# Row maxima and a low pass as pairs of 64-row products in a hybrid attention layer

## The chip, the cores and the metric

One core of one Trainium2 chip runs the whole layer in one launch. The metric is the device time of one execution in microseconds (us). Five engines work from queues of their own, each in order: PE (matmuls; its weight loads are shown as PEld), DVE (elementwise and reductions), ACT (activations, copies), POOL (elementwise on SBUF), SP (issues DMAs). Time before: median 723.49 us of three runs, from 721.98 to 726.29.

## What is computed

One layer of a diffusion backbone: an adaLN-modulated RMSNorm, one input projection, two attention mixers side by side, gates, one output projection. There are 1024 latent tokens, 128 prompt tokens and 128 cached context tokens. Each mixer has 8 query heads of width 64 and 2 key heads, so that four query heads share a key head.

```python
# mixer A: every latent query sees the context and all latents
s = einsum('bqkgd,bskd->bkgqs', qblk, k_all) * d ** -0.5
p = softmax(s);  o_a = einsum('bkgqs,bskd->bqkgd', p, v_all)
# mixer B: context and the neighbours |i-j| <= 128, with one sink logit per head
s = concatenate([sink, s_ctx, s_band]); p = softmax(s)[..., 1:]
o_b = p_ctx @ v_ctx + p_band @ v_band
y = x + gate * (concatenate([o_a * silu(g_a), o_b * silu(g_b)]) @ w_out)
```

The softmax subtracts any number near the row's largest score; the result doesn't depend on which, as long as nothing overflows.

## The kernel before, in words

**Precision.** A number is split into a high part, rounded to fp32r, and a low part, the remainder in fp32r. A product of two split numbers is high x high + high x low + low x high: three fp32r matmuls, or fewer where two share the 128 rows of the array.

**Stages.** First norm, modulation and the gate columns of mixer A; then the queries of both mixers (`query`), keys and values (`key`, `put_keys`), the gate columns of mixer B; then the attention sweep with the output projection strewn into it. In `query` the four pairs of heads of a 128-token tile are transposed, split into `qo[0]` (high) and `qo[1]` (low), and written to DRAM by `put` on ACT's queue: high parts in rows 0 to 63 of `q_dram`, low parts in rows 64 to 127, for each key group 512 columns (four heads x 128 queries).

**Units and slots.** The sweep goes over units `(t, m, g)`: token tile, mixer, key group, in the order A, B, A, B for each tile. A unit of mixer A has nine slots, one for each block of 128 keys; a unit of mixer B has three or four (its window). In a slot the loop at the end calls, in this order: `tick` (what earlier slots put off with `later`), `scores` of this slot (mixer A: two matmuls and an exponential; mixer B: four transposes of ready weights), the work that is due by table, some output products, and `values` of the slot three earlier.

**Work that is due by table.** `u_load` brings a unit's queries as one tile `qt`, 128 rows x 512, five slots ahead. `max_items` finds the row maxima of a mixer A unit: for each of four heads and three groups of three key blocks one product of 384 columns (`pmx`, L858; `kha` holds each key's high part twice, in rows 0 to 63 and 64 to 127, so that queries' high and low parts both meet it) and one reduce on DVE (L859). `finish` then loads the queries' high part again (`qb`), negates the maxima, and `transpose` puts them (`ptm`, L877) as extra rows of `qb`. `weight_items` makes mixer B's weights in natural layout: for each head two products (L915 with the keys' high part, L916 with their low part, `klb`, again stored twice), a masked maximum with the sink on DVE (L919), the exponential with its sum on ACT (L905). Then come the inverses of the sums: reciprocal on DVE, a transpose on PE (`pti`, L967), a copy on ACT (L971).

`MX_AT` and `NAT_AT` are slots counted from the start of another unit: a mixer A unit's maxima lie in the mixer B slots ahead of the previous mixer A unit (-4 to -1) and in that unit's own slots (4 to 8); a mixer B unit's weights in the slots 0 to 3 of the mixer A unit before it. Units 0 and 2 take their maxima earlier, beside mixer B's gate products.

**Accumulators.** PSUM has eight banks of 512 fp32 columns. Two of tag A rotate: each call of `bank("A", ...)` takes the other one, and waits for that one's last reader. All products above (`pmx`, `sn`, `ptm`, `pti`) use tag A; scores use B, value sums C, output products D and E.

Of the kernel before, what the change touches and what calls it, by code (L numbers as in the profile page):

```python
# [39 lines left out]
LOADED = 4  # L40


NAT_AT = (0, 1, 2, 3)
NAT_FIRST = (0, 1, 2, 3)
MX_AT = (-4, -3, -2, -2, -1, 4, 5, 5, 7, 7, 8, 8)
MX_FIRST = (0, 1, 2, 2, 3, 4, 4, 5, 6, 6, 7, 8)
PH_DVE = 0
MX_END = 10
SPLIT_LAG = 2
# [58 lines left out]
def hybrid_step(ctx, tc, x_prompt, x_sample, cache_k_a, cache_v_a, cache_k_b, cache_v_b,  # L108
# [26 lines left out]


    ps = ctx.enter_context(tc.tile_pool(name="ps", bufs=1, space=PSUM))
    BANKS = {"A": 2, "B": 2, "C": 2, "D": 1, "E": 1}
    turn = {"mm": 0, "tr": 0}
# [411 lines left out]
    with tc.tile_pool(name="qt", bufs=2, side="right") as qt:  # L551
# [34 lines left out]
        def query(pq, m, t, tabs, n=1):  # L586

            nm = f"q{m}_{t}"
            pqv = pq.rearrange("p (h d) -> p h d", d=HD)
            v = {}  # L590

            def squares():
                sq = qt.tile([P, 8, HD], F32, tag="sq", name=f"sq{nm}")
                nc.scalar.activation(sq, pqv, AF.Square)  # L594
                ss = qt.tile([P, 8], F32, tag="ss", name=f"ss{nm}")
                nc.vector.tensor_reduce(ss, sq, axis=AX.X, op=ALU.add)
                v["r"] = rsqrt_mean(qt, ss, HD, 8, nm)

            def scale():
                qn = qt.tile([P, 8, HD], F32, tag="qn", name=f"qn{nm}")  # L600
                nc.vector.tensor_tensor(qn, pqv, v["r"].unsqueeze(2).to_broadcast([P, 8, HD]), op=ALU.mult)
                v["qn"] = qn
                if t:
                    v["rot"] = rope_products(qt, qn, 8, *tabs[m], t, nm)

            def rotated():

                qf = qt.tile([P, 4, 2, HD], F32, tag="qf", name=f"qf{nm}", bufs=3)
                out = qf.rearrange("p h g d -> p g h d")
                pair = lambda a: a.rearrange("p (g h) d -> p g h d", g=2)  # L610
                if t:
                    nc.vector.tensor_tensor(out, *(pair(a) for a in v["rot"]), op=ALU.add)
                else:
                    nc.vector.tensor_tensor(
                        out, pair(v["qn"]), gain4[:, 2 * m, :].unsqueeze(1).unsqueeze(1).to_broadcast([P, 2, 4, HD]),
                        op=ALU.mult)
                v["qf"] = qf

            def turned():
                ptq = bank_tr(f"pt{nm}")  # L620
                for h in range(4):
                    nc.tensor.transpose(ptq[:, P * h : P * h + P], v["qf"][:, h].rearrange("p g d -> p (g d)"),
                                        ident_r.bitcast(F32))
                qo = [qt.tile([P, 512], F32R, tag=f"qo{i}", name=f"qo{i}{nm}") for i in range(2)]
                nc.scalar.copy(qo[0], ptq)
                put(qo[0], 0)
                later(1, lambda: low(ptq, qo))

            def low(ptq, qo):
                nc.vector.tensor_tensor(qo[1], ptq, qo[0], op=ALU.subtract)  # L630
                later(1, lambda: put(qo[1], 1))

            def put(part, i):
                for g in range(2):
                    nc.scalar.dma_start(q_dram[t][m][64 * i : 64 * i + 64, 512 * g : 512 * g + 512],
                                       part[64 * g : 64 * g + 64].bitcast(F32))
# [197 lines left out]
    def u_load(i):  # L834
        t, m, g = units[i]
        more = i % QTS > 3
        qt_ = (qp2[0] if more else qp).tile([P, 512], F32R, tag="qt", name=f"qt{i}", bufs=QTS - 4 if more else 4)
        nc.sync.dma_start(qt_.bitcast(F32), q_dram[t][m][:, 512 * g : 512 * g + 512])
        qtile[i] = qt_

    def max_items(i):

        t, m, g = units[i]
        out = []

        def item(h, b):
            if h == 0 and b == 0:
                mxtile[i] = qs.tile([P, 4, 3], F32, tag="mx", name=f"mx{i}", bufs=3)
            mx = mxtile[i]
            lhs = qtile[i][:, P * h : P * h + P]  # L850
            pm = bank("A", f"pmx{i}_{h}_{b}")
            if t == 0:
                for h in range(4):
# [3 lines left out]
            else:  # L857
                nc.tensor.matmul(pm[:, 0:384], lhs, kha[:, g, 3 * b : 3 * b + 3, :], start=True, stop=True)  # L858
                nc.vector.tensor_reduce(mx[:, h, b : b + 1], pm[:, 0:384], axis=AX.X, op=ALU.max)  # L859

        def finish():
            qb_ = qp.tile([68, 512], F32R, tag="qb", name=f"qb{i}", bufs=2)
            nc.sync.dma_start(qb_[0:64, :].bitcast(F32), q_dram[t][m][0:64, 512 * g : 512 * g + 512])
            qbtile[i] = qb_
            mx = mxtile.pop(i)
            mn = m_nat[i // 2 % 2]
# [15 lines left out]
        for h in range(4 if t else 1):  # L882
            for b in range(3 if t > 0 else 1):
                out.append(lambda h=h, b=b: item(h, b))
        return out, finish

    def weight_items(i):
# [20 lines left out]
        def item(h):  # L908
            p0, p1_ = window(t)
            n = P * (p1_ - p0)  # L910
            if h == 0:
                first(n)
            lhs = qtile[i][:, P * h : P * h + P]
            s = bank("A", f"sn{i}_{h}")[:, 0:n]
            nc.tensor.matmul(s, lhs, khb[:, g, p0:p1_, :], start=True, stop=False)  # L915
            nc.tensor.matmul(s, lhs, klb[:, g, p0:p1_, :], start=False, stop=True)  # L916
            m0 = P if t == 1 else 0

            nc.vector.tensor_tensor_reduce(s, s, mask[:, m0 : m0 + n], -1.0, nsink[:, 4 * g + h : 4 * g + h + 1],  # L919
                                           op0=ALU.add, op1=ALU.min, accum_out=v["nm"][:, h : h + 1])  # L920
            later(1, lambda: exp(h, s, -1.0))

        def prompt():
            first(P)
# [55 lines left out]
        return ([lambda h=h: item(h) for h in range(4)] if t else [prompt]), finish  # L980


    wo_raw, wo_parts, wo_big = {}, {}, {}
# [231 lines left out]
    for i, (t, m, g) in enumerate(units):  # L1215
# [8 lines left out]
        else:  # L1224
            items, done = weight_items(i)
            at = [start[i - 1] + j for j in (NAT_AT if i > 1 else NAT_FIRST)] if t else [start[i] - PROMPT_LEAD]
            end = at[-1] + 1
# [95 lines left out]
```

## Time and profile before

| | us |
|---|---|
| median of three runs | 723.49 |
| lowest and highest run | 721.98, 726.29 |
| the profiled execution, first to last instruction (span) | 721.3 |
| first and last `ptm` of the sweep over latent tiles, from the start of the span | 353.4, 662.2 |
| one unit of mixer A and one of mixer B in it | 23.84 to 23.87 |

The profile is of one execution, and its time is the span; the page gives no other time for it. In its lists an instruction is named by line, engine, operation, and `out<-in` with the program's tile names without buffer numbers; `128*64` means 128 rows by 64 columns of the array, `128x512` partitions by elements, `x4` four of them merged. In a timeline the two figures ahead are start and length in us. A matmul's length is its latency; the next one begins sooner, so the distance between two starts tells what one costs. In brackets stands how long the engine was idle before, and what released it.

### The profile page before, as it was taken

How to read it: one execution, taken by the hardware profiler on the slowest of the kernel's cores; microseconds unless marked ns; L12 is line 12 of the kernel's file. 1: busy time of each engine (PE TensorE's matmuls, PEld its weight loads, DVE VectorE, ACT ScalarE, POOL GpSimd, SP SyncE). 2: the span in 40 equal slices, each digit the busy share in tenths (PEclk: the TensorE clock that was granted, in tenths of full speed). 3: DMA queues.
4: the chain of work that ended last, by engine and by line, in shares of the span. 5: the costliest groups of instructions: out<-in, count | busy, mean ns of one | idle time of the engine just before them, and what ended most of it. 6: DMA issues, size and time to landing. Idle time of an engine off the chain costs nothing. (4 is left out here: it accounts for less than half of the span.)

```text
span 721.3 us, 10622 instructions
## 1 busy us (share of the span) xinstructions
PE 698.3 (97%) x3524; PEld 559.7 (78%) x3524; DVE 457.6 (63%) x1007; ACT 411.7 (57%) x829; POOL 335.3 (46%) x355
## 2 busy tenths in 40 slices
PE   5999999999999999999999999999999999999997
PEld 2678988877777788977788888888888888887865
DVE  3466147875675872745866677577666775775653
ACT  5355411411232451158778877877787778877770
POOL 3456013332322340236666555655575557555751
PEclk9999999999999999999999999999999999999999
DMA  8961373348435115440321222121212221212323
GB/s 344 346 219 59 121 278 86 79 94 276 121 85 142 45 60 171 139 143 23 103 67 45 73 67 88 44 81 52 87 54 59 66 87 45 81 53 87 103 65 119
DMA packets 53159, 78.56 MB, mean 109 GB/s; under 512 B 6569, under 2 KB 25449, under 8 KB 52081
## 3 DMA queue, kind: packets, MB, share of 16 engines
q1 hardware_dynamic: 44928, 65.96, 28.1%
q10 hardware_dynamic: 8176, 11.94, 6.3%
q8 instruction: 28, 0.46, 0.3%
q14 instruction: 27, 0.21, 0.1%
HBM read 58.69 MB, written 19.18 MB: 108 GB/s over the span
## 5 line engine op out<-in xcount | busy, mean ns | idle before, releaser
L1108 POOL TENSOR_TENSOR pl<-pe,ph 128x512 fp32r<-128x512 f32 x130 | 167.6, 1292 | 144.7 <-DVE nm L919 67.5
L859 DVE TENSOR_REDUCE mx<-pmx 128x1 f32<-128x384 f32 x192 | 101.4, 552 | 59.5 <-PE pmx L858 58.1
L1100 ACT ACTIVATE pe<-st 128x512 f32<-128x512 f32 x146 | 86.8, 594 | 28.0 <-PE st L1098 27.1
L1104 ACT CAST ph<-pe 128x512 fp32r<-128x512 f32 x146 | 90.6, 621 | 4.8
L1118 PE MATMUL pv<-ph,v_hi 128*128 128x512 f32 x208 | 83.2, 400 | 2.2 <-DVE spare L1142 2.2
L1121 PE MATMUL pv<-pl,v_hi 128*128 128x512 f32 x208 | 82.6, 397 | 0.0
L173 POOL TENSOR_TENSOR rs_q<-ms_q,mhalf 128x8 f32<-128x8 f32 x18 | 34.8, 1931 | 82.1 <-DVE ms_q L171 82.1
L1189 PE MATMUL po<-wo,ogh 128*128 128x512 f32 x216 | 72.5, 394 | 0.2 <-DVE yt L1196 0.2
L919 DVE CUSTOM_DVE_ANT_0 sn<-sn,mask,nsink 128x512 f32<-128x512 f32 (+1 forms) x64 | 46.3, 724 | 38.3 <-PE sn L916 36.5
L858 PE MATMUL pmx<-kha,qt 128*128 128x384 f32 x192 | 61.0, 363 | 0.4 <-ACT pen L905 0.2
L1097 PE MATMUL st<-qt,kha 128*128 128x512 f32 x144 | 58.3, 405 | 1.5 <-ACT pe L1100 0.8
L1098 PE MATMUL st<-qb,kla 68*128 68x512 f32 x144 | 57.6, 400 | 1.1 <-DVE qb L878 1.1
L1120 PE MATMUL pv<-ph,v_lo 128*64 128x512 f32 x146 | 57.9, 396 | 0.0
L1121 PEld LDWEIGHTS pv<-pl,v_hi 128*128 128x128 f32 x208 | 39.4, 189 | 16.7 <-issue 0.2
L905 ACT ACTIVATE pen<-sn,nm 128x512 f32<-128x512 f32 (+2 forms) x72 | 45.0, 626 | 6.5 <-DVE nm L919 3.1
L1093 ACT CAST ph<-st 128x512 fp32r<-128x512 f32 x62 | 36.4, 587 | 19.9 <-PE st L1092 18.7
L1118 PEld LDWEIGHTS pv<-ph,v_hi 128*128 128x128 f32 x208 | 39.4, 189 | 10.5 <-ACT ogh L1154 2.4
L1189 PEld LDWEIGHTS po<-wo,ogh 128*128 128x128 f32 x216 | 40.0, 188 | 6.8 <-DVE yt L1196 0.6
L1094 DVE TENSOR_TENSOR pl<-st,ph 128x512 fp32r<-128x512 f32 x62 | 42.5, 686 | 2.3 <-ACT ph L1093 1.5
L1189 PE MATMUL po<-wo,ogl 128*128 128x512 f32 x108 | 42.6, 394 | 0.0
L594 ACT ACTIVATE sqq<-pq 128x512 f32<-128x512 f32 x18 | 10.8, 599 | 53.3 <-DMA qd<-qo0q 14.4
L858 PEld LDWEIGHTS pmx<-kha,qt 128*128 128x128 f32 x192 | 35.5, 190 | 6.2 <-DVE mx L859 1.4
(216 smaller groups left out, 1700.2 us busy)
## 6 DMA issues: line engine op xcount, KB each, us to landing
qt<-qd SPq DMA_DIRECT2D x36, 256.0 KB, 3.1
wm<-in_w_mod_ss_dram SPq DMA_DIRECT2D x8, 1024.0 KB, 5.1
qd<-qo0q ACTq DMA_DIRECT2D x36, 128.0 KB, 2.4
qd<-qo1q ACTq DMA_DIRECT2D x36, 128.0 KB, 2.4
sgl<-gd SPq DMA_DIRECT2D x36, 128.0 KB, 2.1
out_dram<-yt SPq DMA_DIRECT2D x17, 256.0 KB, 2.1
xn<-in_x_sample_dram SPq DMA_DIRECT2D x8, 512.0 KB, 7.0
wg<-in_w_mod_g_dram SPq DMA_DIRECT2D x4, 1024.0 KB, 7.9
```

Source lines behind the costliest of these rows:

```text
L858: nc.tensor.matmul(pm[:, 0:384], lhs, kha[:, g, 3 * b : 3 * b + 3, :], start=True, stop=True)
L859: nc.vector.tensor_reduce(mx[:, h, b : b + 1], pm[:, 0:384], axis=AX.X, op=ALU.max)
L919: nc.vector.tensor_tensor_reduce(s, s, mask[:, m0 : m0 + n], -1.0, nsink[:, 4 * g + h : 4 * g + h + 1], op0=ALU.add, op1=ALU.min, accum_ou ...
L1097: nc.tensor.matmul(s, kh, qtile[i], start=True, stop=False)
L1098: nc.tensor.matmul(s, kl, qbtile[i], start=False, stop=True)
L1100: nc.scalar.activation(pe, s, AF.Exp)
L1104: nc.scalar.copy(ph, pe)
L1108: nc.gpsimd.tensor_tensor(pl, pe, ph, op=ALU.subtract)
L1118: nc.tensor.matmul(pv, two, ph, start=(b == 0), stop=False)
L1120: nc.tensor.matmul(pv[0:64, :], vl, ph, start=False, stop=False)
L1121: nc.tensor.matmul(pv, two, pl, start=False, stop=last)
L1189: nc.tensor.matmul(po[n], a, wo_parts[KT * n + k][lo], start=(k == KS[0] and p == 0), stop=(k == KS[-1] and p == 2))
```

## The change

- In DRAM a query tile is now `[4, 64, 2, 256]`: two heads' high part, the same heads' low part, the next two heads' high part, their low part, in pieces of 256 numbers. `u_load` issues two DMAs: rows 0 to 63 of `qt` get the low part of heads 0 and 1 and the high part of heads 2 and 3, rows 64 to 127 the high part of heads 0 and 1 and the low part of heads 2 and 3. All full 128-row products are sums over the same pairs of rows as before.
- `halves(q)` names two heads, q and q + 2, and the row at which each one's high part starts: 64 and 0.
- The maxima of mixer A now take the queries' high part alone: one product over 64 rows for each of the two heads, at row 64 and at row 0 of the array, into two banks, and one reduce over both.
- Mixer B's product with the keys' low part takes the queries' high part alone, in the same pairs. The product with the keys' high part stays whole.
- The two banks of tag A are one tile, `two`. A pair writes both; single users still take turns.
- The tables have half as many entries: maxima in slots -4, -3, -2, 4, 6, 8, mixer B's weights in slots 0 and 2.

```diff
-NAT_AT = (0, 1, 2, 3)
-MX_AT = (-4, -3, -2, -2, -1, 4, 5, 5, 7, 7, 8, 8)
+NAT_AT = (0, 2)
+MX_AT = (-4, -3, -2, 4, 6, 8)
...
-    q_dram = [[dram.tile([P, 1024], F32, name=f"qd{t}_{m}") for m in range(2)] for t in range(NT)]
+    q_dram = [[dram.tile([4, HD, 2, 256], F32, name=f"qd{t}_{m}") for m in range(2)] for t in range(NT)]
...
+    two = ps.tile([P, 2, 512], F32, name="two")
     def bank(tag, name):
+        if tag == "A":
+            turn["A"] += 1
+            return two[:, turn["A"] % 2]
...
-        nc.sync.dma_start(qt_.bitcast(F32), q_dram[t][m][:, 512 * g : 512 * g + 512])
+        for a, parts in ((0, slice(1, 3)), (HD, slice(0, 4, 3))):
+            nc.sync.dma_start(qt_[a : a + HD].bitcast(F32).rearrange("d (s n) -> d s n", s=2),
+                              q_dram[t][m][parts, :, g, :].rearrange("s d n -> d s n"))
+    def halves(q):
+        return (q, HD), (q + 2, 0)
...
-                nc.tensor.matmul(pm[:, 0:384], lhs, kha[:, g, 3 * b : 3 * b + 3, :], start=True, stop=True)
-                nc.vector.tensor_reduce(mx[:, h, b : b + 1], pm[:, 0:384], axis=AX.X, op=ALU.max)
+            for n, (h, a) in enumerate(halves(q)):
+                nc.tensor.matmul(two[:, n, 0:384], qtile[i][a : a + HD, P * h : P * h + P],
+                                 kha[a : a + HD, g, 3 * b : 3 * b + 3, :], start=True, stop=True, tile_position=(a, 0))
+            nc.vector.tensor_reduce(mx.rearrange("p (n q) b -> p q b n", n=2)[:, q, b], two[:, :, 0:384], axis=AX.X,
+                                    op=ALU.max)
...
-            nc.tensor.matmul(s, lhs, khb[:, g, p0:p1_, :], start=True, stop=False)
-            nc.tensor.matmul(s, lhs, klb[:, g, p0:p1_, :], start=False, stop=True)
+            for j, (h, a) in enumerate(halves(q)):
+                nc.tensor.matmul(two[:, j, 0:n], qtile[i][:, P * h : P * h + P], khb[:, g, p0:p1_, :], start=True,
+                                 stop=False)
+            for j, (h, a) in enumerate(halves(q)):
+                nc.tensor.matmul(two[:, j, 0:n], qtile[i][a : a + HD, P * h : P * h + P], klb[a : a + HD, g, p0:p1_, :],
+                                 start=False, stop=True, tile_position=(a, 0))
```

The order of instructions at three places follows; line numbers of the changed kernel are larger by some 12 to 19. First PE, where mixer B's slots begin (first slot, up to the second one's maxima), before:

```order
L1092 MATMUL st_0_5536<-ident_r,pen_5339 128x128 x4
L858 MATMUL pmx_0_0_5545<-kha,qt_5437 128x384
L1118 MATMUL pv_5415<-ph_6_5473,v_hi 128x512
L1120 MATMUL pv_5415<-ph_6_5473,v_lo 64x512
L1121 MATMUL pv_5415<-pl_6_5474,v_hi 128x512
L967 MATMUL pti_5551<-ident_r,inv_5343 4x128
L1092 MATMUL st_1_5556<-ident_r,pen_5339 128x128 x4
L858 MATMUL pmx_0_1_5569<-kha,qt_5437 128x384
```

and PE in the same unit with the change:

```order
L1111 MATMUL st_0_5333<-ident_r,pen_5150 128x128 x4
L870 MATMUL two<-kha,qt_5244 128x384 x2
L1137 MATMUL pv_5223<-ph_6_5275,v_hi 128x512
L1139 MATMUL pv_5223<-ph_6_5275,v_lo 64x512
L1140 MATMUL pv_5223<-pl_6_5276,v_hi 128x512
L986 MATMUL two<-ident_r,inv_5154 4x128
L1111 MATMUL st_1_5352<-ident_r,pen_5150 128x128 x4
L870 MATMUL two<-kha,qt_5244 128x384 x2
```

The single products became pairs in the same places; the transpose of the inverses stays between two of them, all on the tile `two`. On DVE, from the last mixer A slot into the same mixer B slots, before:

```order
L859 TENSOR_REDUCE mx_5248<-pmx_3_1_5523 128x1
L859 TENSOR_REDUCE mx_5248<-pmx_3_2_5526 128x1
L954 RECIPROCAL inv_5343<-sum_5341 128x4
L859 TENSOR_REDUCE mx_5544<-pmx_0_0_5545 128x1
L1094 TENSOR_TENSOR pl_0_5538<-st_0_5536,ph_0_5537 128x512
L869 TENSOR_REDUCE m_5566<-mx_5248 128x4
L872 TENSOR_SCALAR m_nat_108<-m_5566 128x4
L859 TENSOR_REDUCE mx_5544<-pmx_0_1_5569 128x1
```

and DVE with the change:

```order
L872 TENSOR_REDUCE mx_5067<-two 128x2
L973 RECIPROCAL inv_5154<-sum_5152 128x4
L872 TENSOR_REDUCE mx_5341<-two 128x2
L1113 TENSOR_TENSOR pl_0_5335<-st_0_5333,ph_0_5334 128x512
L884 TENSOR_REDUCE m_5362<-mx_5067 128x4
L887 TENSOR_SCALAR m_nat_109<-m_5362 128x4
L872 TENSOR_REDUCE mx_5341<-two 128x2
```

Each reduce now reads two banks and gives two maxima. Last, PE in the second and third slot of a mixer A unit, with mixer B's scores, before:

```order
L1097 MATMUL st_1_5353<-qt_4853,kha 128x512
L1098 MATMUL st_1_5353<-qb_5268,kla 128x512
L915 MATMUL sn_1_5362<-khb,qt_5233 128x512
L916 MATMUL sn_1_5362<-klb,qt_5233 128x512
L1189 MATMUL po_0_5006<-wo_6_3231,ogh_5213 128x512
L1189 MATMUL po_0_5006<-wo_6_3230,ogl_5214 128x512
L1189 MATMUL po_0_5006<-wo_7_3255,ogh_5213 128x512
L1118 MATMUL pv_5324<-ph_2_5281,v_hi 128x512
L1121 MATMUL pv_5324<-pl_2_5282,v_hi 128x512
L1097 MATMUL st_2_5376<-qt_4853,kha 128x512
L1098 MATMUL st_2_5376<-qb_5268,kla 128x512
L915 MATMUL sn_2_5385<-khb,qt_5233 128x512
```

and PE there with the change:

```order
L1116 MATMUL st_1_5167<-qt_4704,kha 128x512
L1117 MATMUL st_1_5167<-qb_5086,kla 128x512
L1208 MATMUL po_0_4843<-wo_6_3200,ogh_5034 128x512
L1208 MATMUL po_0_4843<-wo_6_3199,ogl_5035 128x512
L1208 MATMUL po_0_4843<-wo_7_3218,ogh_5034 128x512
L1137 MATMUL pv_5135<-ph_2_5099,v_hi 128x512
L1140 MATMUL pv_5135<-pl_2_5100,v_hi 128x512
L1116 MATMUL st_2_5185<-qt_4704,kha 128x512
L1117 MATMUL st_2_5185<-qb_5086,kla 128x512
L929 MATMUL two<-khb,qt_5051 128x512 x2
L932 MATMUL two<-klb,qt_5051 128x512 x2
```

The second slot no longer has a head; the third has two, whose half products are the last pair of rows.

More of the change, by code (lines that the diff above doesn't have):

```diff
@@ L634, in put @@
                 for g in range(2):
[L635 to L636 removed]
+                    nc.scalar.dma_start(
+                        q_dram[t][m][i::2, :, g, :].rearrange("s d n -> d s n"),
+                        part[64 * g : 64 * g + 64].bitcast(F32).rearrange("d (s n) -> d s n", s=2))
             for d, f in zip(QUERY_LAST if (m, t) == (1, 0) else QUERY_AT, (squares, scale, rotated, turned)):
@@ L844, in max_items, with item @@
         out = []
-        def item(h, b):
-            if h == 0 and b == 0:
+        def item(q, b):
+            if q == 0 and b == 0:
                 mxtile[i] = qs.tile([P, 4, 3], F32, tag="mx", name=f"mx{i}", bufs=3)
             mx = mxtile[i]
-            lhs = qtile[i][:, P * h : P * h + P]
-            pm = bank("A", f"pmx{i}_{h}_{b}")
             if t == 0:
+                pm = bank("A", f"pmx{i}")
                 for h in range(4):
@@ L880, in transpose @@
                                     diag.unsqueeze(2).to_broadcast([4, 4, P]), op=ALU.mult)
-        for h in range(4 if t else 1):
-            for b in range(3 if t > 0 else 1):
-                out.append(lambda h=h, b=b: item(h, b))
+        for q in range(2 if t else 1):
+            for b in range(3 if t else 1):
+                out.append(lambda q=q, b=b: item(q, b))
         return out, finish
@@ L978, in rows @@
                                   r_dram[i // 2].rearrange("(c s) n -> s c n", s=2)[s : s + 1].to_broadcast([HD, 2, P]))
-        return ([lambda h=h: item(h) for h in range(4)] if t else [prompt]), finish
+        return ([lambda q=q: item(q) for q in range(2)] if t else [prompt]), finish
     wo_raw, wo_parts, wo_big = {}, {}, {}
@@ L1226, in hybrid_step @@
             at = [start[i - 1] + j for j in (NAT_AT if i > 1 else NAT_FIRST)] if t else [start[i] - PROMPT_LEAD]
-            end = at[-1] + 1
+            end = at[-1] + (2 if t else 1)
         if i >= LOADED:
```

27 lines of the change are left out of this document (14 added, 13 removed).

## The prediction

> **What bounds the kernel now.** I read the page's busy times first:
>
> ```profile
> PE 698.3 (97%) x3524; PEld 559.7 (78%) x3524; DVE 457.6 (63%) x1007; ACT 411.7 (57%) x829; POOL 335.3 (46%) x355
> ```
>
> Then the windows, over the query projections and over one whole period of the attention sweep (from one transpose of maxima, `ptm`, to the next):
>
> ```profile
> 105.00:205.00 100.00, 99.22 (x473) 77.02 (x472) 73.38 (x142) 26.93 (x48) 31.17 (x16) 1.00 0.49 137
> 520.22:544.09 23.87, 23.87 (x116) 19.18 (x115) 17.67 (x37) 18.74 (x37) 14.09 (x15) 1.00 0.27 85
> ```
>
> The columns are length, then busy time of PE, PEld, DVE, ACT and POOL, granted clock, DMA share, GB/s. PE is busy for the whole of a period and at full clock; ACT is next with 18.74 of 23.87 us. A period holds one unit of mixer A (nine slots) and one of mixer B (four). So PE's instructions set the time, and what is taken from them counts, as far as nothing else then makes PE wait. A busy PE is not yet proof of that, so I read the starts of neighbouring matmuls, which are the pace:
>
> ```profile
> 500.59 0.39 PE L915 MATMUL sn<-khb,qt 128*128 128x512 f32 x1
> 500.82 0.40 PE L916 MATMUL sn<-klb,qt 128*128 128x512 f32 x1
> ...
> 507.50 0.40 PE L1118 MATMUL pv<-ph,v_hi 128*128 128x512 f32 x1
> 507.73 0.40 PE L1120 MATMUL pv<-ph,v_lo 128*64 128x512 f32 x1
> 507.97 0.40 PE L1121 MATMUL pv<-pl,v_hi 128*128 128x512 f32 x1
> ...
> 508.68 0.51 PE L858 MATMUL pmx<-kha,qt 128*128 128x384 f32 x2
> 509.02 0.39 PE L1189 MATMUL po<-wo,ogl 128*128 128x512 f32 x1
> ```
>
> A matmul of 512 columns holds PE for 0.23 us (500.59 to 500.82), two of 384 columns for 0.34 (508.68 to 509.02), 0.17 each. The second figure of a row, 0.39, is latency and is not paid by the next one.
>
> **What the change takes from PE.** The twelve row-maximum products of a mixer A unit (L858, 384 columns) become six pairs, each half over 64 rows. If two halves run side by side, a pair costs 0.17 and a stagger, taken as 0.01: 0.18 in place of 0.34 to 0.35. Sixteen units with six pairs are 96 pairs, 96 x 0.16 = **15.4 us**. In mixer B two full low passes (L916) become one pair: 0.24 in place of 0.46 for 24 pairs of 512 columns, 0.16 less for the 8 pairs of 384 at the window's ends: 24 x 0.22 + 8 x 0.16 = **6.6 us**. Together 22.0 us.
>
> No row of this profile has a matmul at a row offset; the nearest are the column tiles of the gate rows, four at a time:
>
> ```profile
> 158.73 0.39 PE L250 MATMUL pq<-whiqb,h 128*128 128x512 f32 x1
> 159.05 1.92 PE L573 MATMUL pgate<-wg,sil32g 128*32 128x512 f32 x16
> 160.90 0.66 PE L622 MATMUL ptq<-ident_r,qfq 128*128 128x128 f32 x4
> 161.31 0.47 PE L248 MATMUL pq<-whiqb,h 128*128 128x512 f32 x1
> ```
>
> Sixteen products of 512 columns end within 1.92 us, though at 0.23 each they would hold PE for 3.7. So tiles at different positions do run together. The same rows show a price: the block begins 0.32 after the matmul ahead of it, 0.09 more than the usual pace, and a matmul whose weights were not loaded under the one ahead takes 0.47 (161.31) where its like takes 0.39 (158.73). Against this, the 128*64 product at 507.73 stands between 128*128 ones with 0.23 and 0.24 on either side: there a change of tile costs nothing. The block that pays has plain fp32 operands (`wg`, `sil32g`), the 128*64 product has fp32r ones (`ph`, `v_lo`), as the new pairs have. Bounds for a pair's extra cost are thus 0 (507.73) and, on both sides, 0.09 for the start and 0.08 for such a weight load in the open, 0.34 in all. I take 0, since the fp32r row is the nearer one.
>
> The Trainium skill ("TensorEngine Tiling (Array Packing)", Tiling Modes, Key Properties) says that changing the tiling mode drains the TensorE, which speaks against pairs strewn one by one among full products. By that rule the row at 507.73 should show a gap, and it does not; it is a column mode, though, and no row here shows a row mode. What a drain would do is the second rival.
>
> **What takes it back.** Both accumulators of tag A become one tile, `two`, and every pair fills both banks. Before, a product took the bank that its predecessor had not; now each use waits until the last reader of both is done. Where mixer B's slots begin, the orders printed above show what that does. The transpose of the inverses (`pti` before, `two<-inv` now) stands as close behind the maxima as it did, but now overwrites what their reduce still reads, and its copy must in turn end before the next pair. On DVE one reduce of 768 elements stands where one or two of 384 did, with the same subtraction (`pl`) and small steps between. The times of this place before the change (start, length), on PE:
>
> ```profile
> 514.50 0.51 PE L858 MATMUL pmx<-kha,qt 128*128 128x384 f32 x2
> ...
> 515.53 0.60 PE L1092 MATMUL st<-ident_r,pen 128*128 128x128 f32 x4
> 515.89 0.42 PE L858 MATMUL pmx<-kha,qt 128*128 128x384 f32 x1
> ...
> 516.86 0.27 PE L967 MATMUL pti<-ident_r,inv 128*4 128x128 f32 x1
> ...
> 517.32 0.42 PE L858 MATMUL pmx<-kha,qt 128*128 128x384 f32 x1
> ...
> 520.22 0.22 PE L877 MATMUL ptm<-ident_r,m_nat 128*4 128x128 f32 x1
> ```
>
> on DVE
>
> ```profile
> 514.87 1.02 DVE L859 TENSOR_REDUCE mx<-pmx 128x1 f32<-128x384 f32 x2 [0.97 <-PE pmx L858]
> 515.81 0.17 DVE L954 RECIPROCAL inv<-sum 128x4 f32<-128x4 f32 x1
> 516.35 0.56 DVE L859 TENSOR_REDUCE mx<-pmx 128x1 f32<-128x384 f32 x1 [0.37 <-PE pmx L858]
> 516.83 0.68 DVE L1094 TENSOR_TENSOR pl<-st,ph 128x512 fp32r<-128x512 f32 x1
> 517.42 0.16 DVE L869 TENSOR_REDUCE m<-mx 128x4 f32<-128x12 f32 x1
> 517.61 0.42 DVE L872 TENSOR_SCALAR m_nat<-m 128x4 fp32r<-128x4 f32 x1
> 517.95 0.55 DVE L859 TENSOR_REDUCE mx<-pmx 128x1 f32<-128x384 f32 x1
> ```
>
> and on ACT
>
> ```profile
> 517.17 0.25 ACT L971 COPY spare<-pti 4x128 f32<-4x128 f32 x1 [0.41 <-PE pti L967]
> ```
>
> What a longer reduce takes I read from the groups by form, of 384 and of 512 elements (mean ns behind the busy time):
>
> ```profile
> L859 DVE TENSOR_REDUCE mx<-pmx 128x1 f32<-128x384 f32 x192 | 101.4, 552 | 59.5 <-PE pmx L858 58.1
> ...
> L596 DVE TENSOR_REDUCE ssq<-sqq 128x8 f32<-128x512 f32 x18 | 12.3, 684 | 12.3 <-ACT sqq L594 12.1
> ```
>
> A reduce takes 0.55 us for 384 elements and 0.68 for 512, so about 0.95 for 768 (an estimate on that line). A reader starts 0.46 after a matmul whose weights load in the open (515.89 to 516.35), and a release reaches PE some 0.04 later. On the clock of these rows:
> 1. Pair at 514.50, reduce 514.89 to 515.84. The next pair gets there at 515.74 (one product fewer ahead) and goes at 515.88: waits 0.14.
> 2. Its reduce runs 516.34 to 517.30. `pti` gets there at 516.86 and goes at 517.34: waits **0.48**.
> 3. Its copy ended 0.56 after it began, now 517.90. The next pair, 0.46 behind `pti`, gets there at 517.80 and goes at 517.94: 0.14.
> 4. DVE does `pl`, the small maximum and `m_nat` until 518.41 (1.1 from one reduce to the next's start, as from 516.83 to 517.95), then the reduce until 519.36. From a pair to the next slot PE takes 0.97 (515.89 to 516.86), and 0.36 of transposes; it is there at 519.27 and goes at 519.40: 0.13.
> 5. Behind the next `pl` (0.57 until its follower starts) that reduce runs 519.93 to 520.88. PE takes 0.97 and two output products, gets to `ptm` at 520.83 and goes at 520.92: 0.09.
>
> That is 0.98 us a period (`ptm` 0.70 later than at 520.22, with two products fewer on the way). Behind the waiting products in PE's queue stand the value products, which nothing else delays, so the wait is paid in full. In every second period a tile's output is finished at this place:
>
> ```profile
> 538.42 0.69 DVE L1196 TENSOR_TENSOR yt<-po,yt 128x512 f32<-128x512 f32 x1
> 539.03 1.01 DVE L859 TENSOR_REDUCE mx<-pmx 128x1 f32<-128x384 f32 x2
> ```
>
> One period of 23.87 after 514.50 the pair stands at 538.37; its reduce starts at 539.03 and ends at 539.98, so step 1 costs 0.41 and all 1.25. Fourteen of the sixteen mixer A units have such pairs (the first two take their maxima beside the gate products, where nothing stands close): 14 x 1.12 = **15.7 us**.
>
> In mixer B's scores, two sink minima and two exponentials now follow one another on the same two banks, with two slots between. I count nothing there, since a whole slot without such a pair lies between; the upper bound is one more wait like step 2's, 0.48 x 16 = 8 us, the lower none. Shorter reduces in sum (six of 0.95 for twelve of 0.55) and the copies that DVE and ACT make are not on the path.
>
> The queries lie in memory in pieces of 256 numbers, where 512 stood together, and each tile is loaded by two DMAs in place of one. SP issues 36 more; the writes stand on ACT's queue as before. The cover is PE, busy for 99.22 of 100 us where they are written with DMA at 0.49, and a lead of five slots where they are read. Bounds are 0 and, should a landing be late once a unit, some 0.1 x 36 = 4 us; I take 0.
>
> **The sum.** 22.0 off, 15.7 back: 6.3 us less than the profiled 721.3, which is 715.0. The runs' median, 723.49, lies 2.2 above that span (the lowest of them, 721.98, 0.7), so on its scale 717.2.
>
> **Rivals.**
> *The waits are covered.* Should DVE's reduce cost hardly more than one of 384, or the waits overlap with ones that I count twice, only some 5 us come back: 706. Against it: step 2 needs only one row, 552 ns and its length. 0.08.
> *Each pair drains PE (slower).* At either end of a pair PE empties and loads weights in the open, as the fp32 blocks do: 0.18 + 0.34 = 0.52 in place of 0.35, and 0.57 in place of 0.46: 96 x 0.17 + 32 x 0.11 = 20 us more. Waits on the banks shrink to some 0.5 a period, 7 us. 723.5 + 27 = 750. It decides from 0.05 us a pair on, since 6.3 us over 128 pairs is no more than that. For it: 159.05; against it: 507.73. 0.20.
> *The change doesn't do what it says.* If the row halves run one behind the other, PE saves nothing, and the waits, a little smaller, remain: 0.9 x 14 = 13 us more, 736. If only the second half's weights are late (a load in the open is about 0.1, from four transposes in 0.36 at 515.53), a pair costs 0.28: some 9 us off, 15 back, 729. For both: no row pair is in this trace; against: sixteen column tiles in 1.92. Together 0.20.
>
> **How the numbers follow.** Forecast as summed, with 711 to 722 for its own range (waits of 0.8 to 1.4 a period), 0.52. With 0.08, 0.20 and 0.20 for the rivals: faster by over 0.5% means below 719.9, which is most of the forecast's case and the first rival, 0.47. Within 0.5%, about what a measurement of this kernel can tell from no change: the forecast's upper end and a part of the late weights, 0.18. Slower: 0.35. The range leaves out most of the draining case, and a little below: 707 to 744.
>
> **What would show it.** Right: two products of `two<-kha` starting within 0.02 us, and the next full one 0.18 later; PE idle about 0.5 us before `two<-inv`, released by DVE's reduce; a period of 23.2 to 23.7 us. Wrong: 0.3 us or more between the matmul ahead and a pair (drain); 0.1 or 0.17 between its halves; idle time before L929 released by ACT; reduces of 768 far from 0.95.

## The result, and the profile after

| | us | ratio to before, 95% interval |
|---|---|---|
| before, median of 4 runs beside the changed kernel (721.98 to 726.39) | 724.89 | |
| changed kernel, median of 4 runs (787.46 to 792.68) | 789.54 | 1.0904, 1.0865 to 1.0944 |
| profiled execution (span), before and after | 721.3 and 789.1 | |

The change makes the kernel slower by 9%. The forecast was 717.2, its range 707 to 744: the sign was wrong and the time lies far outside. The busy times and one whole period of the sweep, from one transpose of maxima to the next (columns as before):

```profile
PE 740.5 (94%) x3524; PEld 536.4 (68%) x3524; DVE 455.0 (58%) x911; ACT 409.3 (52%) x829; POOL 334.5 (42%) x355
```

```profile
518.86:545.18 26.32, 26.08 (x116) 17.32 (x115) 18.00 (x31) 18.47 (x37) 13.96 (x15) 1.00 0.23 71
```

PE executes the same 3524 matmuls, of which 256 now cover half the rows, and a period has the same 116. Yet PE is busy 26.08 us in a period where it was busy 23.87. This isn't visible idleness: PE "works" longer on less. The timeline of PE, around a pair and at the place that the forecast's step 2 spoke of (L870 is the pair of maxima, L1208 the output product, L1137 to L1140 the value products, L986 the inverses' transpose):

```profile
529.56 0.39 PE L1116 MATMUL st<-qt,kha 128*128 128x512 f32 x1
529.79 0.40 PE L1117 MATMUL st<-qb,kla 68*128 68x512 f32 x1
530.12 0.44 PE L870 MATMUL two<-kha,qt 64*128 64x384 f32 x2
530.49 0.73 PE L1208 MATMUL po<-wo,ogh 128*128 128x512 f32 x2
531.06 0.40 PE L1137 MATMUL pv<-ph,v_hi 128*128 128x512 f32 x1
...
541.24 0.27 PE L986 MATMUL two<-ident_r,inv 128*4 128x128 f32 x1 [0.20 <-DVE mx L872]
```

The two halves do run side by side: the records put 3 ns between their starts, and the merged row is 0.44 long. But the pair begins 0.33 after the product ahead (0.23 is the pace), the next product comes 0.37 later (0.18 was expected), and the two output products behind it take 0.57 instead of 0.46 (530.49 to 531.06). So 1.27 us pass from 529.79 to 531.06; before, 0.23 + 0.35 + 0.46 = 1.04 did.

The rest of the loss lies where the forecast did not look. The list of PE's waits (sum, times, longest) has a first row that the kernel before has no counterpart of:

```profile
PE two L253 <- ACT sqq L599: 12.3, 3, 5.9
```

L253 is a projection product of the queries, ACT's L599 squares a projected tile. In windows of 10 us around two of the three waits, after and then before (columns as above, the clock behind POOL):

```profile
140.00:150.00 10.00, 4.34 (x22) 3.38 (x20) 9.26 (x18) 5.61 (x11) 1.94 (x1) 0.85 0.37 88
150.00:160.00 10.00, 9.74 (x37) 7.91 (x38) 3.90 (x8) 0.79 (x2) 1.94 (x1) 0.81 0.07 17
180.00:190.00 10.00, 5.25 (x26) 4.13 (x24) 5.69 (x12) 1.19 (x2) 1.94 (x1) 0.90 0.81 226
```

```profile
140.00:150.00 10.00, 9.87 (x48) 7.83 (x47) 9.93 (x19) 4.95 (x10) 2.92 (x2) 1.00 0.28 65
150.00:160.00 10.00, 10.00 (x55) 7.54 (x57) 6.48 (x14) 1.78 (x3) 3.52 (x3) 1.00 0.41 94
180.00:190.00 10.00, 10.00 (x57) 6.96 (x56) 7.46 (x15) 1.77 (x3) 3.88 (x2) 1.00 0.45 135
```

PE stands still for more than half of one window and nearly half of another; the granted clock then falls. The timeline of PE and ACT there, after the change:

```profile
142.21 4.25 ACT L238 CAST whiqb<-rawqb 128x512 fp32r<-128x512 f32 x8
...
143.52 0.39 PE L255 MATMUL two<-whiqa,h 128*128 128x512 f32 x1
143.75 0.60 PE L627 MATMUL ptq<-ident_r,qfq 128*128 128x128 f32 x4
146.35 0.58 ACT L630 CAST qo0q<-ptq 128x512 fp32r<-128x512 f32 x1
...
148.32 1.25 ACTq L640 DMA_DIRECT2D qd<-qo1q  x2
149.61 0.60 ACT L599 ACTIVATE sqq<-two 128x512 f32<-128x512 f32 x1 [2.67 <-DVE wloqb L240]
150.26 0.79 PE L253 MATMUL two<-whiqb,h 128*128 128x512 f32 x1 [5.91 <-ACT sqq L599]
150.85 0.63 PE L254 MATMUL two<-wloqb,h 128*128 128x512 f32 x1
151.28 0.63 PE L255 MATMUL two<-whiqb,h 128*128 128x512 f32 x1
```

The product at 150.26 writes one half of `two`. The squares at 149.61 read the other half; they stand in ACT's queue behind eight weight casts, a cast of the queries and the issue of the queries' DMAs. As two tiles the banks were independent. As one tile, each write to it waits for each reader of it. By the first gate product of mixer B the kernel is 20.9 us late (280.0 instead of 259.1), by the first `ptm` of the sweep over latent tiles 33.8 (387.2 instead of 353.4). From there to the last one it loses another 30.7 (339.5 instead of 308.8), and 3.3 at the end.

### The profile page after: what moved, and what is told of

Same layout as the page of the kernel before. It is cut to its first block, busy times and chain, and to the rows that moved or that the text cites. A ratio compares the mean times of both kernels' runs of the same rounds, so it can differ in the third digit from the quotient of the medians.

```text
span 789.1 us, 10552 instructions
## 1 busy us (share of the span) xinstructions
PE 740.5 (94%) x3524; PEld 536.4 (68%) x3524; DVE 455.0 (58%) x911; ACT 409.3 (52%) x829; POOL 334.5 (42%) x355
## 2 busy tenths in 40 slices
DMA packets 64104, 78.57 MB, mean 100 GB/s; under 512 B 7145, under 2 KB 46761, under 8 KB 63025
## 5 line engine op out<-in xcount | busy, mean ns | idle before, releaser
L872 DVE TENSOR_REDUCE mx<-two 128x2 f32<-128x768 f32 x96 | 92.1, 959 | 78.7 <-PE two L870 67.0
L1137 PE MATMUL pv<-ph,v_hi 128*128 128x512 f32 x208 | 88.5, 426 | 3.2 <-DVE spare L1161 3.2
L1140 PE MATMUL pv<-pl,v_hi 128*128 128x512 f32 x208 | 83.0, 399 | 0.0
L1208 PE MATMUL po<-wo,ogh 128*128 128x512 f32 x216 | 77.0, 415 | 0.2 <-DVE yt L1215 0.2
L938 DVE CUSTOM_DVE_ANT_0 two<-two,mask,nsink 128x512 f32<-128x512 f32 (+1 forms) x64 | 46.4, 725 | 45.5 <-PE two L932 44.4
L920 ACT ACTIVATE pen<-two,nm 128x512 f32<-128x512 f32 (+2 forms) x72 | 44.6, 625 | 32.9 <-DVE nm L938 29.3
L1137 PEld LDWEIGHTS pv<-ph,v_hi 128*128 128x128 f32 x208 | 39.4, 190 | 21.4 <-issue 10.9
L1140 PEld LDWEIGHTS pv<-pl,v_hi 128*128 128x128 f32 x208 | 39.7, 191 | 17.3 <-issue 0.6
L1208 PEld LDWEIGHTS po<-wo,ogh 128*128 128x128 f32 x216 | 38.4, 188 | 13.5 <-issue 7.8
L1208 PE MATMUL po<-wo,ogl 128*128 128x512 f32 x108 | 45.2, 418 | 0.0
L870 PE MATMUL two<-kha,qt 64*128 64x384 f32 x192 | 42.4, 437 | 1.0 <-DVE mx L872 1.0
L630 ACT CAST qo0q<-ptq 128x512 fp32r<-128x512 f32 x18 | 10.6, 587 | 55.6 <-PE ptq L627 48.8
L412 POOL TENSOR_TENSOR h<-hf,h 128x256 fp32r<-128x256 f32 (+2 forms) x32 | 28.3, 903 | 23.6 <-DVE h L411 23.6
```

The lines of the kernel that those rows point to most:

```text
L872: nc.vector.tensor_reduce(mx.rearrange("p (n q) b -> p q b n", n=2)[:, q, b], two[:, :, 0:384], axis=AX.X, op=ALU.max)
L1137: nc.tensor.matmul(pv, two, ph, start=(b == 0), stop=False)
L1140: nc.tensor.matmul(pv, two, pl, start=False, stop=last)
L1208: nc.tensor.matmul(po[n], a, wo_parts[KT * n + k][lo], start=(k == KS[0] and p == 0), stop=(k == KS[-1] and p == 2))
```

## The experiments

My theory after the profile: three losses of about the same size. (1) A pair of 64-row products costs more around it than it saves. (2) The shared tile makes products wait in the sweep. (3) It makes them wait in the projections. Rivals: the new layout of the queries in DRAM with its additional DMAs; fewer active rows as such; the order of the work. All times are medians; the kernel before, beside each batch, took 723.25, 723.35 and 723.39.

| label | kernel | us | ratio to before, 95% | period, us |
|---|---|---|---|---|
| e1_one_tile | before, the two banks as one tile | 850.53 | 1.1746, 1.1717 to 1.1776 | 30.7 |
| e2_layout | before, the queries' new layout | 723.74 | 1.0007, 0.9991 to 1.0023 | 23.9 |
| e3_banks_early | changed, banks apart until the sweep | 766.46 | 1.0599, 1.0567 to 1.0631 | 26.3 |
| e4_whole | e3 with whole products, no pairs | 758.06 | 1.0473, 1.0452 to 1.0495 | 26.0 |
| e5_rows64 | before, maxima over 64 rows, single | 774.08 | 1.0706, 1.0688 to 1.0723 | 27.0 |
| e6_rows68 | before, maxima over 68 rows, single | 724.42 | 1.0014, 1.0003 to 1.0025 | 23.9 |
| e7_double | e3 with each pair issued twice | 782.56 | 1.0826, 1.0806 to 1.0846 | 27.3 |
| e8_max_only | e3 with whole low passes | 765.13 | 1.0581, 1.0563 to 1.0599 | 26.3 |
| e9_own_banks | changed, banks apart throughout | 754.09 | 1.0432, 1.0414 to 1.0449 | 25.7 |
| e10_own_whole | e9 with whole products | 727.96 | 1.0061, 1.0044 to 1.0078 | 24.1 |

### The shared tile alone, and the layout alone

`e1_one_tile` is the kernel before with one edit:

```diff
-    BANKS = {"A": 2, "B": 2, "C": 2, "D": 1, "E": 1}
-    turn = {"mm": 0, "tr": 0}
+    BANKS = {"B": 2, "C": 2, "D": 1, "E": 1}
+    turn = {"mm": 0, "tr": 0, "A": 0}
+    two = ps.tile([P, 2, 512], F32, name="two")
...
+        if tag == "A":
+            turn["A"] += 1
+            return two[:, turn["A"] % 2]
```

> The kernel before with one edit: the two banks of tag A are the halves of one tile, used in turn as before; no pair, no other table. Theory 1 (the early stages lose their time because a write to one half of the tile waits for the reader of the other half): 15 to 25 us slower than before in the stages up to the sweep, with the same PE waits released by ACT's squares of the queries as in the changed kernel, and some more in the sweep. Rival (the smaller DMA pieces of the queries delay ACT's queue): no change, within 2 us of before.

It took 850.53. The early part came as expected: first gate product at 278.0, 18.9 late. In the sweep far more was lost than I expected, a period of 30.7 us. Its timeline of PE shows the wait by itself:

```profile
507.32 0.42 PE L862 MATMUL two<-kha,qt 128*128 128x384 f32 x1
508.39 0.44 PE L862 MATMUL two<-kha,qt 128*128 128x384 f32 x1 [0.65 <-DVE mx L863]
508.67 0.62 PE L1193 MATMUL po<-wo,ogh 128*128 128x512 f32 x2
```

Two products that write different halves, and had stood 0.17 apart, now stand 1.07 apart: the second waits for the reduce of the first. No data passes between them.

`e2_layout` is the kernel before with the changed kernel's `q_dram` and its DMAs:

```diff
-    q_dram = [[dram.tile([P, 1024], F32, name=f"qd{t}_{m}") for m in range(2)] for t in range(NT)]
+    q_dram = [[dram.tile([4, HD, 2, 256], F32, name=f"qd{t}_{m}") for m in range(2)] for t in range(NT)]
...
-        nc.sync.dma_start(qt_.bitcast(F32), q_dram[t][m][:, 512 * g : 512 * g + 512])
+        for a, parts in ((0, slice(1, 3)), (HD, slice(0, 4, 3))):
+            nc.sync.dma_start(qt_[a : a + HD].bitcast(F32).rearrange("d (s n) -> d s n", s=2),
+                              q_dram[t][m][parts, :, g, :].rearrange("s d n -> d s n"))
```

> The kernel before with the changed layout of the queries in DRAM alone (pieces of 256 numbers, two loads a tile); all products stay whole. Theory 1: within 2 us of before. Rival (DMA pieces): 15 to 25 us slower, all of it before the sweep.

723.74: no difference that can be measured, though the page counts 64104 DMA packets where the kernel before has 53159. This rival is out.

### The early stages

`e3_banks_early` is the changed kernel with two separate banks until the sweep begins, and `two` from there on:

```diff
-    two = ps.tile([P, 2, 512], F32, name="two")
+    two = None
+    psa = ExitStack()
+    early = psa.enter_context(tc.tile_pool(name="psa", bufs=1, space=PSUM))
...
+        if tag == "A" and two is None:
+            return early.tile([P, 512], F32, tag=tag, name=name, bufs=2)
...
+    psa.close()
+    late = ctx.enter_context(tc.tile_pool(name="late", bufs=1, space=PSUM))
+    two = late.tile([P, 2, 512], F32, name="two")
```

> The changed kernel, with two banks of their own for tag A until the sweep, and the one tile only from there. Theory 1: 20 to 25 us faster than the changed kernel, 764 to 770. Rival (DMA pieces): as the changed kernel, 789.

766.46, 23.1 us less than the changed kernel; the first gate product is back at 258.4 and the period stays at 26.3. So (3) is shown, with its price. The waits for ACT's squares, with the 5.91 at 150.26, are gone with the shared tile, and so is the fall of the clock behind them: it is 1.00 in every window of 10 us from 140 to 210.

### The pairs against whole products, with the shared tile

`e4_whole` is e3 with all 128 rows in each product, and the same for the low pass:

```diff
-                nc.tensor.matmul(two[:, n, 0:384], qtile[i][a : a + HD, P * h : P * h + P],
-                                 kha[a : a + HD, g, 3 * b : 3 * b + 3, :], start=True, stop=True, tile_position=(a, 0))
+                nc.tensor.matmul(two[:, n, 0:384], qtile[i][:, P * h : P * h + P], kha[:, g, 3 * b : 3 * b + 3, :],
+                                 start=True, stop=True)
```

> As the run before it, but every half product over 64 rows is a whole one over 128 rows: same order, same two banks, same reduces of 768. Theory 2 (in the sweep the price is PE emptying and loading weights in the open at both ends of each pair): a pair of whole products costs 0.35 us where the half pair costs 0.58, so 20 to 25 us faster than the run before it, and the waits on the banks alone, 10 to 16 us, remain against the kernel before. Rival (the sweep loses by the waits on the two banks): hardly faster than the run before it, or slower, since PE then streams twice the columns.

Only 8.4 us came off, not 20 to 25, and 758.06 is still 35 above the kernel before, where 10 to 16 were expected to remain. PE's own waits show little; the wait stands at the weight loads (PEld). From the timeline of e4_whole:

```profile
501.01 0.40 PE L1124 MATMUL st<-qb,kla 68*128 68x512 f32 x1
...
501.43 0.30 PEld L877 LDWEIGHTS two<-kha,qt 128*128 128x128 f32 x2 [0.46 <-ACT pen L927]
501.43 0.62 PE L877 MATMUL two<-kha,qt 128*128 128x384 f32 x2
...
501.89 0.62 PE L1215 MATMUL po<-wo,ogh 128*128 128x512 f32 x2
...
505.14 0.40 PE L1124 MATMUL st<-qb,kla 68*128 68x512 f32 x1
505.14 0.42 PEld L877 LDWEIGHTS two<-kha,qt 128*128 128x128 f32 x2
...
505.38 0.51 PE L877 MATMUL two<-kha,qt 128*128 128x384 f32 x2
505.73 0.40 PE L1215 MATMUL po<-wo_big,ogl 128*128 128x512 f32 x1
```

At 505.38 nothing is late: the weight load begins 0.24 ahead of the pair, under the product before it (505.14), and the pair follows 0.24 behind that product and takes 0.35. At 501.43 even the weight load has waited and begins together with the pair, in the open; the pair follows 0.42 behind and takes 0.46 (to 501.89). That is 0.29 more, and no idle time is printed on PE's row. The list of PEld's waits from 400 to 640 us, about nine periods, has the sums:

```profile
PEld two L993 <- DVE mx L879: 7.1, 9, 0.8
PEld two L936 <- ACT pen L927: 5.9, 9, 0.7
PEld two L877 <- ACT pen L927: 4.2, 9, 0.5
PEld two L877 <- DVE mx L879: 3.5, 18, 0.2
...
PEld two L899 <- DVE mx L879: 2.9, 9, 0.3
```

23.6 us in all, 2.6 a period. In the kernel before, the same list has no row of a tag A bank. The row of L936 is mixer B's next pair waiting for the exponential that reads the pair before it.

### What a 64-row product costs, without pairs and without the shared tile

`e5_rows64` and `e6_rows68` are the kernel before with one number changed in the maxima: the products stay single and take rows 0 to 63 (the queries' high part), or 0 to 67.

```diff
-            lhs = qtile[i][:, P * h : P * h + P]
+            lhs = qtile[i][0:HD, P * h : P * h + P]
...
-                nc.tensor.matmul(pm[:, 0:384], lhs, kha[:, g, 3 * b : 3 * b + 3, :], start=True, stop=True)
+                nc.tensor.matmul(pm[:, 0:384], lhs, kha[0:HD, g, 3 * b : 3 * b + 3, :], start=True, stop=True)
```

> The kernel before with one edit: each row-maximum product takes the queries' high part alone, over 64 rows, one by one (no pairs, two banks in turn as before). Theory 2 (a change between 128-row and 64-row products empties PE): eight stretches of such products in a unit, each 0.10 us at its start and 0.2 at its end more, so some 2.4 us a unit, 30 to 40 us slower than before. Rival (the price belongs to two products at once, or to the two banks): within 3 us of before.

> As the run before it, but over 68 rows, the high part and four rows of the low part, as L1098 has it: fewer active rows than 128, but not a 64-row tile. Theory 2 in the form that the tile's height is what empties PE: within 3 us of before. Rival form (any product with fewer rows than its neighbours empties it): as slow as the run before it.

64 rows: 50.7 us slower, more than the 30 to 40 expected. 68 rows: 1.1 slower, 0.14%. So a product with fewer active rows than its neighbours costs nothing as such; what costs is the step from a 128-row tile of the array to a 64-row one and back. The trace of e5_rows64 on PE:

```profile
517.62 0.40 PE L1098 MATMUL st<-qb,kla 68*128 68x512 f32 x1
517.95 0.61 PE L858 MATMUL pmx<-kha,qt 64*128 64x384 f32 x2
518.50 0.50 PE L1189 MATMUL po<-wo_big,ogh 128*128 128x512 f32 x1
518.84 0.40 PE L1189 MATMUL po<-wo_big,ogl 128*128 128x512 f32 x1
```

Here two 64-row products stand one behind the other. 0.33 passes ahead of them (+0.10), 0.55 until the next full product (0.35 for two of 384 columns, +0.20), and 0.34 until the one behind it (+0.11): 0.41 in all. The 192 maxima of this trace stand in 135 such stretches of one to three; 135 x 0.41 = 55, and 50.7 was measured. The Trainium skill ("TensorEngine Tiling (Array Packing)", Tiling Modes, Key Properties) says that a change of the tiling mode drains the TensorE; these rows agree for the 64-row tile. A 68-row product among 128-row ones keeps the pace (0.24 from 511.61 to 511.85 in `e10_own_whole`, below), and so does not act as a change of mode.

`e7_double` is e3 with each pair of maxima issued twice, back to back:

```diff
-            for n, (h, a) in enumerate(halves(q)):
+            for n, (h, a) in [*enumerate(halves(q))] * 2:
```

> The changed kernel with banks of its own early (as e3), and each pair of row-maximum products issued twice, back to back, with the same result. Theory 2: the price is paid once for a stretch of 64-row products, so the second pair costs 0.17 to 0.2 us: 96 x 0.18 = 17 us more than e3. Rival (each pair pays for itself): 96 x 0.58 = 56 us more.

16.1 us more than e3, which is 96 x 0.17. In its timeline of PE:

```profile
514.12 0.40 PE L1124 MATMUL st<-qb,kla 68*128 68x512 f32 x1
514.45 0.62 PE L877 MATMUL two<-kha,qt 64*128 64x384 f32 x4
515.00 0.73 PE L1215 MATMUL po<-wo,ogh 128*128 128x512 f32 x2
```

The four products take 0.55, where one pair takes 0.37 (530.12 to 530.49 in the changed kernel). So the second pair costs only 0.18, and the price is paid once per stretch, not per product.

`e8_max_only` is e3 with whole low passes in mixer B:

```diff
-                nc.tensor.matmul(two[:, j, 0:n], qtile[i][a : a + HD, P * h : P * h + P], klb[a : a + HD, g, p0:p1_, :],
-                                 start=False, stop=True, tile_position=(a, 0))
+                nc.tensor.matmul(two[:, j, 0:n], qtile[i][:, P * h : P * h + P], klb[:, g, p0:p1_, :], start=False,
+                                 stop=True)
```

> As e3, but mixer B's low pass runs as whole 128-row products again; only the row maxima are pairs. Theory 2: a low-pass pair costs 0.63 us where two whole products cost 0.46, so this is 4 to 8 us faster than e3. Rival (pairs of 512 columns gain): 3 to 7 us slower than e3.

1.3 us faster than e3, where 4 to 8 were expected; the two intervals overlap. With the shared tile, the low-pass pairs cost nothing that can be told here.

### The pairs without any shared tile

`e9_own_banks` is the changed kernel, order and pairs included, with a bank and a reduce of its own for each half. `e10_own_whole` is the same with whole products. The edit of e9:

```diff
-            for n, (h, a) in enumerate(halves(q)):
-                nc.tensor.matmul(two[:, n, 0:384], qtile[i][a : a + HD, P * h : P * h + P],
...
-            nc.vector.tensor_reduce(mx.rearrange("p (n q) b -> p q b n", n=2)[:, q, b], two[:, :, 0:384], axis=AX.X,
-                                    op=ALU.max)
+            two = [bank("A", f"pmx{i}_{q}_{b}_{n}") for n in range(2)]
+            for n, (h, a) in enumerate(halves(q)):
+                nc.tensor.matmul(two[n][:, 0:384], qtile[i][a : a + HD, P * h : P * h + P],
...
+            for n, (h, a) in enumerate(halves(q)):
+                nc.vector.tensor_reduce(mx[:, h, b : b + 1], two[n][:, 0:384], axis=AX.X, op=ALU.max)
```

> The changed kernel with its order and its pairs, but each half in a bank of tag A of its own, with a reduce of 384 for each (no shared tile anywhere). Theory: without waits the pairs pay their price in full, 96 x 0.235 = 22.5 us for the maxima and some 0.17 x 32 = 5.5 us for the low passes, so some 28 over before: about 751, period near 25.4. Rival: the pairs are cheap where nothing else waits, and the wait on the shared tile is what lengthened them: below 735. Second rival: the change's order itself (two products in a slot, with both banks) costs as much as the shared tile: then near e3_banks_early, 766.

> The same, with whole 128-row products in place of the half pairs: what is left of the change is the query layout and the order. Theory: the 35 us of e4_whole are the shared tile's, so this is back at the time before, 721 to 728. Rival: the order alone costs some of them, since two products of one slot take both banks: 735 to 758.

754.09 and 727.96, close to 751 and at the end of 721 to 728. Between the two kernels only the height of the tiles differs. The timeline of PE in e10_own_whole, then in e9_own_banks:

```profile
511.61 0.40 PE L1115 MATMUL st<-qb,kla 68*128 68x512 f32 x1
511.85 0.51 PE L867 MATMUL pmx<-kha,qt 128*128 128x384 f32 x2
512.20 0.62 PE L1206 MATMUL po<-wo,ogh 128*128 128x512 f32 x2
```

```profile
532.67 0.40 PE L1115 MATMUL st<-qb,kla 68*128 68x512 f32 x1
533.00 0.45 PE L867 MATMUL pmx<-kha,qt 64*128 64x384 f32 x2
533.37 0.50 PE L1135 MATMUL pv<-ph,v_hi 128*128 128x512 f32 x1
533.71 0.40 PE L1137 MATMUL pv<-ph,v_lo 128*64 128x512 f32 x1
```

The pair costs 0.33 + 0.37 + 0.34 = 1.04 (532.67 to 533.71), the whole products 0.24 + 0.35 + 0.23 = 0.82 (0.23 is the pace of the product behind them): the pair is 0.22 dearer, the saved product included. Nothing waits for a bank here. The medians of these distances over all pairs of both traces give 0.217 for a pair of maxima and 0.165 for a low-pass pair, and 96 x 0.217 + 32 x 0.165 = 26.1 us, which is what was measured between the two kernels. The low passes have 5.3 of it, where e8_max_only showed 1.3 with the shared tile; that difference isn't taken apart here.

The weight loads at the same places, in `e10_own_whole` and then in `e9_own_banks`, show how the price comes about:

```profile
511.62 0.43 PEld L867 LDWEIGHTS pmx<-kha,qt 128*128 128x128 f32 x2
512.03 0.36 PEld L1206 LDWEIGHTS po<-wo,ogh 128*128 128x128 f32 x2
```

```profile
533.00 0.19 PEld L867 LDWEIGHTS pmx<-kha,qt 64*128 64x128 f32 x2 [0.37 <-issue]
533.37 0.19 PEld L1135 LDWEIGHTS pv<-ph,v_hi 128*128 128x128 f32 x1 [0.19 <-issue]
533.48 0.14 PEld L1137 LDWEIGHTS pv<-ph,v_lo 128*64 128x64 f32 x1
```

Between whole products, a load begins under the product ahead (511.62 for the products at 511.85, 512.03 for the one at 512.20). Around the pair of 64-row tiles two loads do not: the pair's begin with the pair (533.00), and the next full product's begins with that product (533.37). The product behind that one then starts 0.11 late, as whole products do in e4_whole behind a load in the open (0.46 instead of 0.35).

### The loss put together

| part | from | us |
|---|---|---|
| order of the work (two products in a slot, half the entries) and layout | e10_own_whole over before | 4.6 |
| pairs in place of whole products, banks apart | e9_own_banks over e10_own_whole | 26.1 |
| shared tile in the sweep, with pairs (and one reduce in place of two) | e3_banks_early over e9_own_banks | 12.4 |
| shared tile in the early stages | changed kernel over e3_banks_early | 23.1 |
| sum | | 66.2 |

Beside it stand 64.7 us by the changed kernel's own runs of before; the difference of 1.5 is that of the two medians of before. The parts depend on their order: the shared tile costs 30.1 with whole products (e4_whole over e10_own_whole) and 12.4 with pairs. That fits a pair whose weights load in the open anyway and so loses less by waiting, but no run separates it. No version here beats the kernel before; the best, with the new layout alone, is the same.

## Why the prediction was wrong, step by step

- **What bounds the kernel**: right. PE sets the time, and all that was lost was lost on PE.
- **"If two halves run side by side", 0.18 for a pair**: right as to the halves, which start 3 ns apart and share the array.
- **"Bounds for a pair's extra cost are thus 0 (507.73) and ... 0.34 in all. I take 0, since the fp32r row is the nearer one"**: this step failed. The rows of e9_own_banks give 0.22 over whole products, so 0.22 + 0.17 = 0.39 over the 0.18 assumed, above even the upper bound. The bound had the right parts, a late start and a weight load in the open on each side, 0.17 a side; measured are 0.10 ahead of the pair and 0.30 behind it, and both loads do stand in the open. In place of 22.0 us off came 26.1 on, an error of 48. The row chosen as nearest (a 128*64 product, free on both sides) has narrower columns but all 128 rows; e5_rows64 shows that the height of the tile is what counts, with fp32r operands too, and e6_rows68 that a smaller number of active rows is not. The gate products' block, which was set aside for its plain fp32 operands, was the row with the right sign. The forecast's own sign of being wrong, 0.3 us or more between the matmul ahead and a pair, is there (0.33 at 530.12).
- **Waits on the shared tile, 15.7 us**: right in kind, and near in size by luck. Together with the pairs the tile costs 12.4 us, and a period is 0.6 longer by it (26.3 against 25.7), where 0.98 to 1.25 were forecast. Of the five steps only the second is seen: the transpose of the inverses waits for the reduce of 768 elements, which takes 959 ns, 0.95 by the estimate. From 400 to 640 us of the changed kernel, about nine periods, its weight load waits 5.6 us (1.9 for this transpose in e9_own_banks); on PE's own row 0.20 of each wait is left (541.24), where 0.48 was forecast. The loads of the pairs of maxima wait no more in sum than without a shared tile (14.8 us against 15.6 in e9_own_banks), so the other four steps, 0.50 together, do not appear there; waits of mixer B's scores, put at nothing, stand in their place. With whole products, where much of the wait is held at the weight loads, the shared tile cost 30.1.
- **"I count nothing there" for mixer B's scores**: wrong, and rather near the upper bound of one wait of 0.48 a unit. In the same nine periods of the changed kernel their weight loads wait 4.1 us for ACT's exponential, 0.46 a period; e9_own_banks has no such wait. In e4_whole it is 5.9 us, 0.66 a period. A part of it lies beneath the product ahead.
- **What the change moves**: its order alone costs 4.6 us (e10_own_whole), and the prediction had no term for it.
- **The early stages**: not seen at all, 23.1 us. The sentence "now each use waits until the last reader of both is done" holds for all users of tag A, but was followed only into the sweep; the projections use the same two banks, with ACT as their reader.
- **Layout of the queries and its DMAs at 0**: right (e2_layout).
- **The rival "each pair drains PE", 750, chance 0.20**: right in mechanism. It gave 20 us for the pairs and 7 for the waits, where 26.1 and 12.4 were measured, and like the forecast it lacked the order and the early stages, 27.7 together. A chance of 0.20 was too small, since no row of a 64-row tile stood against it.

## What to carry to other kernels

Count a half-height product by its stretch: here each change to 64-row tiles and back cost 0.41 us, and a pair of 384 columns saves 0.17, so that by these numbers (an estimate, not run) it would take three pairs in a row, six banks, to gain anything. Two buffers that become halves of one tile wait for each other's readers everywhere they are used, so follow each user of the old tag through the whole program, the early stages too, and name the reader and what stands ahead of it in its queue. A product that waits can show no idle time on PE: read the waits of the weight loads beside it.

## What was not expected of the hardware

- A 64-row tile of fp32r operands among 128-row ones costs 0.10 us ahead and 0.31 behind (e5_rows64), once per stretch (e7_double), while 68 active rows cost nothing (e6_rows68) and a 128*64 product goes at the pace of its neighbours. The cost behind the pair falls on two products: the first waits and loads its weights in the open, and the second starts 0.11 late (533.37 and 533.71 in e9_own_banks).
- Where a wait reaches the weight load, a pair of whole products takes 0.46 instead of 0.35 (501.43 and 505.38 in e4_whole), on top of the wait.
- After PE stood still for 5.9 us, products of 512 columns followed each other at 0.43 instead of 0.23 (150.85 to 151.28), and the granted clock was 0.50 from 148 to 152, 0.53 in the next 2 us and 1.00 from 154 on. The early loss is thus more than the sum of its waits.
